# Another order of all engines for one attention kernel on one core

## The chip, the cores and the metric

The kernel runs on one core of a Trainium2 chip. A time is the device time of one execution in microseconds (us); of several, the median is given. The core has five engines that run their own instruction streams and wait for each other by semaphores: TensorE (PE in the profile, its weight loads apart as PEld), VectorE (DVE), ScalarE (ACT), GpSimd (POOL) and SyncE (SP). Transfers are issued by the last two, and a few by ScalarE.

## The reference

Four batches of eight heads, 1024 positions, 64 values per head; float32 in and out.

```python
scale = 1.0 / np.sqrt(head_dim)
scores = scale * np.matmul(q, k.transpose(0, 1, 3, 2))
scores = scores + bias
scores_max = np.max(scores, axis=-1, keepdims=True)
attn = np.exp(scores - scores_max) / (np.sum(np.exp(scores - scores_max), axis=-1, keepdims=True) + 1e-8)
return np.matmul(attn, v).astype(np.float32)
```

## The kernel before

The 32 heads are taken in 16 pairs, in two groups of nine and seven pairs. The work is cut into 256 slots: one head, one block of 128 queries, all 1024 keys. A slot's scores fill two PSUM banks, and three slots (a round) fill the six banks of the tile `pl` (position 0, 1 or 2 in the round says which banks). So a slot can be filled only when the slot three before it in the same position has been read.

No maximum is subtracted. ScalarE takes exp of 227 slots from PSUM to bf16 (line 398), as a rule one slot of 1024 columns per instruction; in a few rounds three slots go in two instructions of 1536 columns. VectorE does the other 29 in six steps (fixed, frac, square, shift, cube, last) that build the bits of a bf16; the first reads the two PSUM banks. TensorE then multiplies the exponentials with v, eight matmuls per slot (line 461), v having a column of ones so that the sum comes along. Up to seven slots share one PSUM bank `po`; VectorE takes its reciprocal (`rs`), scales it (`ob`), and the result is stored from the SP queue. Two such banks, tags xa and xb, alternate, and the transposes of q and k use the same two.

The bias is added once per chunk of queries, when a chain of heads starts: for later heads TensorE adds the difference to the scores that are still in PSUM. For that each pair needs q and k transposed, and once more with the other head's negated: `ko`, `qo` (copied out of PSUM), `ke`, `qe` (half of a pair and half of the next, copied by VectorE for the early pairs, by a transfer for later ones). Early pairs' k and q are first set beside each other in the tile `side`, of which there is one buffer. Loads are issued by GpSimd and convert to bf16; the tiles of pair p are used again by pair p + 4.

What sets the order is a table, `ORDER`, of some 1430 words, one instruction or group each, read in a row; each engine executes its part of that row in that order. The words that the text uses, with a slot's number, or a pair's behind k, q or r:

- F, G: the first and second half of a slot's scores (four matmuls of 128 columns, or two of 256); X: a slot's exp on ScalarE; P, Q: the two wide ones of a round
- f r s h c l: the six steps of a slot on VectorE
- A: a slot's eight output matmuls; a letter a or b behind it opens a new bank with that tag; R, M: reciprocal and evacuation of a bank. `SIZES` says how many slots each bank holds
- S, T, C, D, N: set beside, transpose (with tag a or b), copy out, double on VectorE, negate; V: v's copy
- U, L: ask for the next load. For L it also waits for the VectorE instruction that stands last in the row:

```python
if kind in "LU":
    asked.append(vec.last if kind == "L" else None)
...
gate = asked.pop(0)
if gate is not None:
    tc.add_manual_dep(flight[i], gate.name, DATA, reason="issued beside VectorE's long steps")
```

Of the kernel before, what the change touches and what calls it, by code (L numbers as in the profile page):

```python
# [8 lines left out]
F32 = mybir.dt.float32  # L9
# [13 lines left out]
Dq4p1 F24 X23 G24 Cq5 F25 A13 A16 X24 Dq5p1 G25 Dq5p0 F26 G26 Sk6 A19 X25 f26 F27 G27 Tk6a X27 F28 Ck6 G28 A18 F29
X28 Sq6 G29 F30 R2 G30 M2 Tq6a X29 r26 F31 A21b G31 X30 Cq6 F32 G32 A20 V4 X31 A22 f32 F33 G33 Tk7a X33 F34 Dk6p0 G34
F35 Dq6p0 X34 A28 Ck7 G35 F36 G36 s26 X35 Tq7a F37 Cq7 A27 X36 A29 G37 h26 A23 F38 c26 X37 A24a G38 Dq6p1 F39 A25 X38
R3 V5 F40 G39 Dq7p0 G40 Dq7p1 A30 X39 A35 Dk7p0 F41 M3 A34 X40 G41 l26 A33 Tk8b X41 F42 G42 Ck8 F43 G43 X42 F44 f43
G44 Tq8b X44 F45 G45 Cq8 A31 F46 X45 F47 Dk8p0 G46 Dq8p0 A26b G47 X46 V6 F48 R4 G48 f47 A36 X48 A41 F49 G49 A40 M4
X49 F50 G50 Sr0 F51 r43 G51 X50 A39 Tr0a F52 Cr0 A38 X51 F53 G53 Dr0p3 G52 r47 A37 X53 F54 Dq6p2 G54 R5 X52 F56 Sr1
s43 G56 X54 Tr1a r32 F55 Cr1 X56 G55 Dr0p1 F57 M5 G57 X55 F59 s47 A56a G59 A42 X57 Dr1p1 F58 Dr1p0 G58 f59 A44 X58
A46 F60 G60 A45 s32 X60 F61 G61 h43 A49b R6 F62 h32 X61 G62 c43 F63 G63 A48 X62 r59 L U F64 G64 M6 L A52 A50 X64 c32  # L30
A51 F65 s59 A53 X63 A54a G65 R7 L U U U h47 A55 F67 l32 X65 G67 F66 A60 G66 X67 A62 M7 F68 G68 A61 X66 f68 F70 G70
A63 A58b X70 F69 R8 G69 l43 F71 X69 G71 F73 G73 A67 c47 X71 A57 F72 M8 G72 A66 l47 X72 F74 G74 X73 h59 F75 G75 f74
A47 A65 X75 F76 G76 A64 r74 L U U X76 F77 G77 F78 c59 G78 X77 A73a F79 l59 G79 A72 X79 A70 F80 G80 A69 X78 f80 F82
G82 A43 A75 X82 F81 R9 G81 M9 L F83 G83 X81 F85 f83 G85 A76 A71b X85 F84 G84 r80 L U A81 X84 F86 G86 r68 A78 F88 X86
s74 G88 F87 G87 s68 A59 X87 A82 F89 h68 A77 R10 G89 s80 L U X88 A79 F90 c68 G90 X89 R11 M10 F91 G91 X90 l68 F92 X91
G92 M11 L F93 A89a h80 X92 G93 h74 A68 A84 c74 A85 X93 F94 G94 r83 A86 A90 X94 c80 F95 G95 F96 A32 X95 G96 R12 F97
s83 A93b A87 P96 M12 G97 F98 G98 l74 A88 Tq9a Q96 F99 G99 h83 A92 A91 c83 F100 X99 A74 Cq9 G100 A94 F101 X100 Dq8p1
G101 R13 F102 M13 L Tk9a X101 F103 l80 G102 G103 A96b X102 A101 F104 Ck9 L G104 A97 X103 f104 F105 G105 Tk10a X105
F106 Ck10 G106 F107 G107 X106 Nq9 F108 G108 f107 A80 X108 A100 F109 G109 l83 A95 X109 F110 G110 A99 F111 X110 R14
G111 M14 F112 Tq10a r104 P111 G112 A103b Cq10 L F113 G113 A108 r107 A98 Q111 Tq11a Nq10 F114 Cq11 G114 F115 A106 X114  # L40
s107 L G115 F116 G116 Nq11 A109 X115 s104 F117 G117 Tk12a h104 X117 F118 Ck12 G118 A105 A102 X118 f116 F120 G120
Tk11a X120 F121 Ck11 L G121 F119 G119 X121 F123 f119 G123 A110a A114 X123 F124 G124 R15 F122 M15 X124 G122 F126 c104
L G126 A113 X122 Tq12b r116 F127 G127 X126 s116 L A111 A83 A112 h107 L F125 X127 Cq12 A115 G125 F129 R16 G129 X125
M16 L U F130 G130 c107 Tk13b X129 F128 l104 G128 A121a A126 X130 A123 l107 F132 A127 X128 A117 G132 A120 h116 A118
X132 Ck13 F131 G131 F133 R17 G133 X131 M17 L F135 G135 A124b f135 L X133 F134 G134 A122 A130 X134 r119 F138 G138 F136
X138 G136 F137 f136 L U U U G137 Tk14a X137 F141 G141 A129 Ck14 X141 F139 F140 c116 G139 A137 X139 Tq14a G140 Cq14
F144 X140 F142 G142 l116 L G144 A131 X142 A125 F143 R18 G143 M18 A104a X144 F145 G145 r135 A107 X145 A133 s119 F147
A128 A116 r136 X143 G147 A134 s135 F148 A132 X147 G148 h119 F146 R19 L G146 Nq12 A139b X148 M19 F150 G150 c119 Tq13a
X146 F151 Cq13 L A138 A143 X150 G151 l119 F149 A140 A141 X151 F153 G149 h135 Tq15a s136 L X149 F154 G154 Nq13 G153
A142 Nq14 L X154 F152 Cq15 G152 A119 X153 f152 F157 G157 A148a A145 X157 F156 r152 L G156 F155 G155 X156 R20 F160  # L50
f155 G160 A144 A149 X160 F159 G159 s152 L A147 X159 F158 G158 M20 F163 A146 c135 X158 G163 F162 G162 r155 A156 X163
# [12 lines left out]
G216 A207b F218 X216 A208 l199 G218 A206 F217 X218 F219 G217 c203 G219 A210 X217 R29 F221 f219 G221 A211 X221 F220
G220 M29 F222 G222 X220 F224 f222 G224 A212 A213 X224 F223 G223 r219 F225 X223 G225 F227 r222 A220a A216 X225 s222
F226 G226 A215 h222 G227 P226 F228 R30 s219 A214 G228 A221 M30 A209 Q226 A217 A224b R31 F229 l203 G229 F230 A198 X229
G230 A218 M31 F231 G231 X230 c222 F232 G232 A223 f231 A199 X232 F233 G233 A228 l222 X233 F234 G234 F235 G235 X234
F236 f235 G236 A225 A233a X236 F237 G237 R32 h219 F238 X237 r235 F239 G238 A203 r231 A234 P238 G239 M32 F240 G240
A226 s235 A227 Q238 F241 c219 F242 G241 s231 A232 A222 P241 h235 F243 G243 R33 c235 G242 A239b A238 l219 Q241 A229
A230 F244 G244 l235 F245 A240 X244 G245 F246 G246 M33 A237 X245 F247 f246 G247 A243 A235a X247 F248 G248 h231 A219  # L70
X248 R34 F249 r246 G249 F250 G250 s246 X249 A236 F251 A242 h246 A245 P250 M34 G251 F252 G252 c231 A244 A241 A247b
Q250 l231 F253 F254 A248 G253 A249 R35 c246 X253 F255 G254 M35 A251 G255 X254 l246 A252 A231 A250 X255 A253a R36 A246
M36 A254 A255 R37 M37
"""
SIZES = (6, 7, 7, 7, 7, 7, 5, 6, 6, 7, 7, 7, 7, 7, 7, 7, 7, 7, 7, 7, 7, 7, 7, 7, 7, 7, 7, 7, 7, 5, 7, 7, 7, 7, 7, 7,
         7, 4)


class Recorder:

    def __init__(self, engine):
        self.engine, self.last = engine, None

    def __getattr__(self, name):
        def call(*args, **kwargs):
            i = getattr(self.engine, name)(*args, **kwargs)  # L86
            self.last = i.ins
            return i
        return call
# [3 lines left out]
def kernel(  # L93
# [610 lines left out]
```

## Time and profile before

| what | us |
|---|---|
| median of 3 runs (lowest, highest) | 225.54 (225.21, 225.86) |
| the profiled execution | 225.5 |
| its span, first to last instruction | 223.7 |
| TensorE busy | 214.4 |
| ScalarE busy | 211.9 |
| VectorE busy | 204.9 |
| GpSimd busy | 70.8 |

Busy time of TensorE is modelled, since its matmuls are pipelined; ScalarE's instructions overlap their neighbours by some tenths of a microsecond, so a mean duration is longer than the distance from start to start. A row of a group ends with the idle time of the engine just before the group's instructions and what ended it. The helper that records VectorE's instructions gives all of them line 86, so they are told apart by their tiles.

### The profile page before, as it was taken

To read this page: it belongs to the slowest core of one execution; us is meant where nothing else is said; L and a number is where in the kernel's file an instruction comes from. 1 tells how busy PE (TensorE), PEld (TensorE's weight loads), DVE (VectorE), ACT (ScalarE), POOL (GpSimd) and SP (SyncE) were. 2 spreads that over 40 slices of the span, in tenths; PEclk is the share of its full clock that TensorE was granted. 3 is DMA by queue.
4 is the path that set the end of the run, shared out by engine and by line. 5 is a ranking of instruction groups with operands and counts; after the bars stand their busy time and mean duration, and the time that the engine had idled before them with its cause. 6 is when DMAs were issued, how large, how long until landed. Compare 5 with 4: busy or idle time off the path is not lost.

```text
span 223.7 us, 9044 instructions
## 1 busy us (share of the span) xinstructions
PE 214.4 (96%) x3965; PEld 197.2 (88%) x3965; DVE 204.9 (92%) x354; ACT 211.9 (95%) x227; POOL 70.8 (32%) x90
## 2 busy tenths in 40 slices
PE   7799999999999999999999999999999999999992
PEld 2689989999999999999999889888898999898992
DVE  2679999999999999999998899999999999999992
ACT  2799998999999999999999999999999999999991
POOL 8825347446254555030436542343000000000000
PEclk9999999999999999999999999999999999999999
DMA  6999999999979999788999999999311021130123
GB/s 177 225 205 216 228 234 177 167 149 180 155 109 153 107 118 144 96 121 179 145 192 143 168 115 201 172 145 95 71 45 44 23 65 41 32 85 25 39 71 103
DMA packets 86087, 28.87 MB, mean 129 GB/s; under 512 B 65888, under 2 KB 82784, under 8 KB 86048
## 3 DMA queue, kind: packets, MB, share of 16 engines
q0 software_dynamic: 62880, 14.06, 70.2%
q1 hardware_dynamic: 22464, 13.38, 23.5%
q10 hardware_dynamic: 704, 0.85, 1.3%
q8 instruction: 31, 0.51, 1.0%
q14 instruction: 8, 0.07, 0.1%
HBM read 29.36 MB, written 8.39 MB: 169 GB/s over the span
## 4 chain that ended last, share of the span: by engine, by line
ACT 54%; PE 22%; DVE 11%; DMA 7%; issue 2%; SPq 1%; DVEq 0%
ACT E L398 54%; PE pl L375 12%; PE po L461 6%; DMA out_dram<-ob 3%; DMA dy<-in_k_dram 2%; PE px L276 2%; DMA ke<-ko 2%; DVE ds L86 1%; DVE qe L86 1%; PE pl L372 1%; DVE ko L86 1%; DVE ob L86 1%; DVE side L86 1%; DVE de L86 1%; DVE qo L86 1%
## 5 line engine op out<-in xcount | busy, mean ns | idle before, releaser
L398 ACT ACTIVATE E<-pl 128x1024 bf16<-128x1024 f32 (+2 forms) x223 | 209.0, 1102 | 2.7 <-PE pl L375 2.5
L461 PE MATMUL po<-vall,E 128*128 128x65 bf16 x1816 | 87.5, 194 | 0.7 <-DVE ob L86 0.3
L461 PEld LDWEIGHTS <-E 128*128 128x128 bf16 x1816 | 77.4, 98 | 3.5 <-DVE ob L86 0.9
L375 PE MATMUL pl<-qo,ko 128*128 128x128 bf16 (+1 forms) x752 | 78.1, 239 | 0.6 <-ACT E L398 0.5
L375 PE MATMUL pl<-qe,ke 128*128 128x128 bf16 (+1 forms) x648 | 67.3, 239 | 0.7 <-ACT E L398 0.3
L375 PEld LDWEIGHTS <-ko 128*128 128x128 bf16 x856 | 57.3, 98 | 6.2 <-ACT E L398 2.1
L375 PEld LDWEIGHTS <-ke 128*128 128x128 bf16 x648 | 43.3, 98 | 4.3 <-ACT E L398 1.6
L86 DVE TENSOR_SCALAR dy<-pl 128x1024 int32<-128x1024 f32 x29 | 35.3, 1218 | 3.1 <-PE pl L375 2.9
L86 DVE SCALAR_TENSOR_TENSOR de<-dy,ds 128x1024 uint16<-128x1024 int32 x29 | 34.9, 1214 | 0.1
L213 POOL DMA_DIRECT2D k<-in_k_dram x18 | 16.3, 909 | 28.8 <-PE pl L375 8.2
L86 DVE TENSOR_TENSOR ob<-po,rs 128x448 f32<-128x448 f32 (+3 forms) x38 | 22.8, 599 | 0.4
L213 POOL DMA_DIRECT2D q<-in_q_dram x18 | 16.6, 921 | 20.4 <-DVE ds L86 10.1
L250 POOL DMA_DIRECT2D vall<-in_v_dram x18 | 16.2, 903 | 18.4 <-DMA vall<-in_v_dram 8.0
L86 DVE TENSOR_TENSOR ds<-ds,de 128x1024 f16<-128x1024 f16 x29 | 19.6, 680 | 0.1
L86 DVE TENSOR_TENSOR ds<-de 128x1024 f16<-128x1024 f16 x29 | 19.5, 676 | 0.1
L86 DVE TENSOR_SCALAR de<-dy 128x1024 f16<-128x1024 uint16 x29 | 19.5, 682 | 0.1
L372 PE MATMUL pl<-ident,braw 128*128 128x128 bf16 x136 | 14.1, 228 | 0.0
L86 DVE TENSOR_SCALAR qo<-px,sgn 128x1024 bf16<-128x1024 bf16 (+2 forms) x18 | 12.4, 688 | 1.6 <-PE px L276 1.4
L461 PE MATMUL po<-vall,de 128*128 128x65 bf16 x232 | 12.5, 194 | 0.0
L86 DVE TENSOR_SCALAR de<-de 128x1024 f16<-128x1024 f16 x29 | 12.3, 432 | 0.2
L372 PEld LDWEIGHTS <-braw 128*128 128x128 bf16 x136 | 11.7, 149 | 0.5
L86 DVE COPY ko<-px 128x1024 bf16<-128x1024 bf16 (+1 forms) x16 | 10.6, 666 | 1.2 <-PE px L282 1.1
(54 smaller groups left out, 127.2 us busy)
## 6 DMA issues: line engine op xcount, KB each, us to landing
ke<-ko SPq DMA_DIRECT2D x20, 128.0 KB, 5.5
k<-in_k_dram POOLq DMA_DIRECT2D x18, 128.0 KB, 5.2
q<-in_q_dram POOLq DMA_DIRECT2D x18, 128.0 KB, 4.5
vall<-in_v_dram POOLq DMA_DIRECT2D x18, 128.0 KB, 5.6
out_dram<-ob SPq DMA_DIRECT2D x33, 64.0 KB, 2.9
braw<-in_bias_dram POOLq DMA_DIRECT2D x7, 256.0 KB, 6.0
de<-in_v_dram POOLq DMA_DIRECT2D x7, 256.0 KB, 7.4
out_dram<-ob SPq DMA_DIRECT2D x9, 192.0 KB, 4.1
```

The source lines that it names most:

```text
L86: i = getattr(self.engine, name)(*args, **kwargs)
L213: return nc.gpsimd.dma_start(out=t[:, :, y, :], in_=(qf, kf)[x][pr][:, y].rearrange("p (c d) -> p c d", d=D))
L250: return nc.gpsimd.dma_start(out=vall[:, (2 * pr + t) % VR, :, :D], in_=vf[pr][:, t])
L276: m = nc.tensor.transpose(px[:, c, :], raws[pr, which, c0][:, c].rearrange("p t d -> p (t d)"), ident[:])
L372: m = nc.tensor.matmul(to, braw[:, c1, :].rearrange("p (kp kc) -> p kc kp", kc=NCH)[:, kc, :], ident8[:], start=i == 0 and order[0] == "b" ...
L375: m = nc.tensor.matmul(pl[:, 2 * x + b, i * P:(i + n) * P], kk[:, kc, :], qq[:, c:c + n, :].rearrange("p c q -> p (c q)"), start=i == 0 an ...
L398: read(nc.scalar.activation(E[:, e0:e0 + n].rearrange("p b x -> p (b x)"), pl[:, b0:b0 + n].rearrange("p b x -> p (b x)"), ACTF.Exp, scale ...
L461: nc.tensor.matmul(bank[b][:, banks[b].index(s), :], weights(s, kc), vall[:, slots[s][2] % VR, kc, :], start=first and kc == 0, stop=kc == ...
```

## The change

`ORDER` is another row of nearly the same words, and three banks hold other numbers of slots; the rest of the program is the same, word for word. The slots on VectorE are the same but two: 48 in place of 47 and 224 in place of 222. Rounds 96 and 111 take three exponentials in place of two wide ones. The words that ask for loads are 27 L and 48 U in place of 29 L and 46 U. The description of the change speaks of a search for the mean end over nine courses with drawn disturbances, and of 24 of 42 loads that wait for VectorE; in the built program 27 of these 42 have a wait for VectorE, and before it was 29. Of the table's lines these hold places that the prediction speaks of:

```diff
-Dq1p0 X2 F6 Sk2 G6 Tk2a X6 F5 G5 Sq2 F7 X5 G7 Dk1p1 Tq2b X7 Cq2 F8 G8 F9 G9 V0 X8 F10 Ck2 A0b A2 X9 Dq1p1 A3 Sk3 G10
+Dq1p0 X2 F6 Sk2 G6 Dk1p1 Tk2a X6 F5 Ck2 G5 F7 X5 Sq2 F9 G7 Dq1p1 G9 Dk2p0 X7 F8 G8 Tq2b V0 X8 F10 Cq2 G10 A5a A2 X9
...
-A128 A116 r136 X143 G147 A134 s135 F148 A132 X147 G148 h119 F146 R19 L G146 Nq12 A139b X148 M19 F150 G150 c119 Tq13a
+G145 A107 X145 A133 s135 F147 A132 M18 G147 X143 A131 F148 l116 A138 G148 X147 F146 A134 G146 R19 Tq13a X148 M19 F150
...
-SIZES = (6, 7, 7, 7, 7, 7, 5, 6, 6, 7, 7, 7, 7, 7, 7, 7, 7, 7, 7, 7, 7, 7, 7, 7, 7, 7, 7, 7, 7, 5, 7, 7, 7, 7, 7, 7,
+SIZES = (6, 7, 7, 7, 7, 7, 6, 4, 7, 7, 7, 7, 7, 7, 7, 7, 7, 7, 7, 7, 7, 7, 7, 7, 7, 7, 7, 7, 7, 5, 7, 7, 7, 7, 7, 7,
```

The first place is VectorE's preparation of pairs 1 and 2. `k16_127` and `q16_129` are the loads of k2 and q2, `ko_294` is k1, `qo_325` is q1. Before:

```order
L86 COPY side_333<-k16_127 128x2x8x64
L86 COPY side_357<-q16_129 128x2x8x64
L86 COPY ke_368<-ko_294 64x1024
L86 TENSOR_SCALAR qo_380<-px_370,sgn_91 128x1024
L86 COPY vall_98<-de_131 128x16x64
L86 COPY ko_404<-px_339 128x1024
```

And now:

```order
L86 COPY side_333<-k16_127 128x2x8x64
L86 COPY ke_339<-ko_294 64x1024
L86 COPY ko_355<-px_341 128x1024
L86 COPY side_368<-q16_129 128x2x8x64
L86 TENSOR_SCALAR qe_378<-qo_325 64x384
L86 COPY ke_339<-ko_355 64x1024
L86 COPY vall_98<-de_131 128x16x64
L86 TENSOR_SCALAR qo_409<-px_394,sgn_91 128x1024
```

k1's doubled copy and k2's copy out of PSUM now stand between the two copies that set k2 and q2 beside.

The second place is the same for pair 4: `k16_217` and `q16_219` are its loads, `ko_481` or `ko_475` is k3. Before:

```order
L86 COPY ke_406<-ko_481 64x1024
L86 TENSOR_TENSOR ob_534<-po_408,rs_517 128x384
L86 TENSOR_SCALAR qo_545<-px_524,sgn_91 128x1024
L86 COPY side_561<-k16_217 128x2x8x64
L86 TENSOR_SCALAR qe_442<-qo_545 64x1024
L86 COPY side_594<-q16_219 128x2x8x64
L86 COPY ko_609<-px_576 128x1024
```

And now:

```order
L86 TENSOR_TENSOR ob_524<-po_415,rs_508 128x384
L86 TENSOR_SCALAR qo_536<-px_515,sgn_91 128x1024
L86 COPY side_555<-k16_217 128x2x8x64
L86 COPY ke_357<-ko_475 64x1024
L86 TENSOR_SCALAR qe_453<-qo_536 64x1024
L86 TENSOR_SCALAR qe_586<-qo_536 64x1024
L86 COPY ko_596<-px_576 128x1024
L86 COPY side_617<-q16_219 128x2x8x64
```

k3's doubled copy, which stood ahead of the evacuation, a second copy of q3 and k4's copy out now stand between the two.

The third place is VectorE at slots 80 and 83: their first steps write `dy_1901` and `dy_1949` before, `dy_1908` and `dy_1956` now, and `dy_1796` (now) is slot 74. Before:

```order
L86 TENSOR_SCALAR dy_1901<-pl_102 128x1024
L86 RECIPROCAL rs_1926<-po_1711 128x7
L86 TENSOR_TENSOR ob_1930<-po_1711,rs_1926 128x448
L86 TENSOR_SCALAR dy_1949<-pl_102 128x1024
L86 TENSOR_SCALAR de_1975<-dy_1901 128x1024
```

And now:

```order
L86 TENSOR_SCALAR dy_1908<-pl_102 128x1024
L86 TENSOR_TENSOR ob_1933<-po_1713,rs_1841 128x448
L86 TENSOR_SCALAR de_1945<-dy_1796 128x1024
L86 TENSOR_SCALAR dy_1956<-pl_102 128x1024
L86 TENSOR_SCALAR de_1988<-dy_1956 128x1024
```

The reciprocal has gone ahead of slot 80's first step, and slot 74's second step stands ahead of slot 83's first one.

More of the change, by code (lines that the diff above doesn't have):

```diff
@@ L23 @@
[L23 to L27, printed above, removed]
@@ new lines @@
+X28 Ck6 F29 G29 F30 R2 Dk6p0 G30 X29 F31 M2 Tq6b V4 G31 X30 F32 Cq6 G32 A20a f32 X31 A21 F33 G33 Tk7b X33 Dq6p1 F34
+G34 Dq6p0 A23 Ck7 X34 F35 G35 A28 r26 F36 X35 G36 Dk7p0 F37 G37 s26 Tq7b X36 A27 Cq7 A22 A29 X37 F38 V5 G38 F39 R3
+Dq7p0 G39 X38 A25b h26 F40 M3 G40 A34 X39 c26 A24 F41 A30 Dq7p1 X40 A31 l26 G41 Tk8a X41 F42 F43 Ck8 G42 G43 X42 A26
+f43 F44 G44 Tq8a X44 F45 Cq8 G45 F46 X45 G46 Dk8p0 F47 A35 Dq8p0 A33a V6 X46 G47 F48 R4 G48 M4 A41 X47 F49 Sr0 G49
+f48 A40 A36 X49 F50 G50 Tr0b r43 X50 A38 F51 Cr0 G51 F52 X51 A39 Dr0p3 Dq6p2 F53 G53 r48 A37 X53 G52 F54 R5 r32 G54
@@ new lines @@
+X52 Sr1 F56 s43 G56 X54 Dr0p1 F55 s32 Tr1b X56 M5 G55 F57 h43 G57 X55 Cr1 F59 G59 A42a Dr1p0 A56 X57 Dr1p1 F58 h32
+G58 f59 A46 X58 A44 F60 G60 A45 c32 X60 F61 G61 s48 A47 F62 X61 A54b R6 L U r59 G62 A49 F63 M6 L X62 F64 G64 l32 A50
+X64 A55 G63 A53a h48 A62 X63 F65 R7 c43 G65 F67 G67 M7 X65 A61 c48 L U U A51 A52 F66 s59 X67 G66 F68 G68 A60 X66 f68
+L F70 G70 A58 A63b X70 F69 l43 G69 F71 A57 X69 G71 F73 l48 A67 X71 F72 G72 A66 r68 G73 X72 F74 R8 h59 G74 X73 F75 f74
+L G75 A65 X75 A48 F76 G76 M8 A64 X76 F77 R9 G77 s68 A73a F78 X77 G78 c59 L F79 G79 A69 l59 L U X79 A70 F80 G80 A76
@@ new lines @@
+X78 f80 F82 G82 A72 A75 X82 F81 M9 G81 F83 r74 G83 X81 F85 G85 f83 A43 A71b X85 F84 G84 A81 r83 X84 F86 G86 A78 Dq8p1
+L U F88 X86 s74 G88 F87 G87 s83 A82 X87 A79 h74 L F89 G89 h68 L U A77 X88 A59 F90 R11 R10 c74 G90 X89 F91 M10 G91 X90
+l74 F92 X91 G92 M11 A32a F93 r80 X92 G93 A87 A91 s80 F94 X93 G94 A85 h83 F95 c68 G95 X94 A92 A74 c83 A84 F96 X95 h80
+G96 A89b R12 F97 M12 G97 X96 F98 c80 A90 G98 X97 A86 l68 A88 F99 G99 X98 Tq9a A94 Cq9 F100 X99 G100 A93 l80 A68 F101
+X100 G101 F102 Tk9a R13 X101 M13 G102 F103 Nq9 L G103 A96b X102 Ck9 L F104 G104 A101 f104 A97 X103 F105 G105 Tk10a
@@ new lines @@
+X105 l83 F106 G106 F107 G107 X106 F108 f107 G108 A80 A100 X108 F109 G109 Ck10 A99 X109 F110 G110 r107 A95 F111 X110
+R14 G111 M14 A98a F112 A106 r104 X111 G112 Tq10b A103 X112 Cq10 F113 G113 A109 F114 Nq10 X113 G114 s107 Tq11b F115
+X114 Cq11 G115 F116 G116 h107 L A108 X115 F117 f116 L U G117 Tk12b X117 F118 G118 Ck12 A105 A102 X118 F120 R15 G120
+s104 Tk11b X120 F121 M15 G121 F119 Ck11 L G119 X121 F123 G123 f119 A83a A112 X123 F124 G124 Tq12b c107 X124 F122 Cq12
+G122 F126 A110 X122 l107 L U G126 A114 F127 X126 G127 A113 r119 F125 A111 X127 G125 s119 Tk13b F129 h104 X125 G129
@@ new lines @@
+G150 h135 A141b X146 h136 F151 G151 Cq13 L U U A139 A116 X150 c136 F149 G149 A140 l119 X151 F153 Tq15a X149 F154 Cq15
+G154 G153 A142 Nq13 X154 F152 Nq15 G152 A143 f152 A119 X153 F157 G157 A147a X157 c135 F156 G156 F155 G155 X156 F160
+f155 G160 A145 A144 X160 F159 G159 R20 A146 Nq14 X159 F158 r155 G158 A149 F163 r152 L U U X158 F162 G163 M20 A151
+G162 X163 s155 A148 F161 R21 A153b M21 X162 F166 G166 l135 A156 A150 X166 G161 Tk15a h155 L F165 X161 Ck15 G165 F169
+G169 c155 A159 X165 A161 F164 G164 X169 F168 f164 G168 A154 A160 X168 F172 G172 s152 A162a X172 F167 G167 h152 F171
@@ new lines @@
+l136 A157 X167 G171 A165 F175 G175 c152 X171 A158 F170 R22 A163 M22 G170 X175 A166 A167 l155 F174 A169b X170 G174
+F178 l152 A171 X174 F173 G178 G173 R23 A168 X178 f173 F177 G177 A172 X177 F181 M23 G181 F176 G176 X181 F180 f176 G180
+A152 A175 X180 F184 G184 r173 A174 X184 F179 G179 r176 F183 A181a r164 X179 A178 G183 F187 s173 X183 G187 R24 s176
+F182 G182 X187 h173 A170 F186 s164 G186 X182 c173 F190 A179 M24 X186 F185 l173 G185 A180 A155 X185 G190 F189 h164
+G189 A177 X190 h176 F188 c176 G188 X189 c164 A136b A135 R25 F193 l164 X188 G193 F192 A184 G192 X193 F191 l176 G191
@@ new lines @@
+A187 A185 X191 F196 G196 A183 f196 X192 F194 G194 A186 X194 F195 M25 G195 F199 R26 G199 X195 F197 f199 G197 A182a
+A193 X197 F198 G198 F202 f198 G202 F200 X202 G200 r196 A173 X200 F201 G201 r199 F205 G205 X201 M26 A164 F203 A190
+s199 A189 X205 F204 r198 G204 A192 s196 G203 X204 F208 G208 f203 A194b A188 X208 F207 G207 A197 R27 h196 X207 F206
+G206 M27 F211 A201 h199 X206 A191 s198 G211 A202 F210 r203 X211 A200 G210 A205a c196 A204 X210 F213 l196 G213 F209
+A176 X213 F212 G212 c199 A196 X212 A195 G209 l199 F215 X209 G215 F214 R28 R29 s203 X215 G214 h198 F216 X214 M28 G216
@@ new lines @@
+M29 F218 X216 A211b h203 F217 c198 G218 A210 X218 G217 l198 A207 F219 G219 X217 F221 G221 f219 A212 A208 X221 F220
+G220 c203 F222 X220 G222 F224 r219 G224 A206 X222 f224 F223 G223 A213 A220a X223 F225 R30 r224 G225 A215 X225 F227
+l203 F226 G226 A214 P226 F228 s224 A222 G228 G227 h224 A216 Q226 A221 M30 A209 F229 c224 G229 A218b R31 F230 X229
+l224 G230 F231 G231 A228 X230 F232 f231 G232 A199 A217 X232 F233 G233 s219 F234 A223 X233 M31 G234 F235 r231 G235
+X234 F236 G236 f235 A198 A203 X236 F237 G237 A225a r235 X237 F238 F239 h219 G238 A224 R32 s235 P238 G239 A227 F240
```

61 lines of the change are left out of this document (13 added, 48 removed).

## The prediction

> **What bounds the kernel now.** I read the page's busy shares first, then ScalarE's timeline over the whole span, and then two stretches of that timeline in which nothing is late.
>
> ```profile
> PE 214.4 (96%) x3965; PEld 197.2 (88%) x3965; DVE 204.9 (92%) x354; ACT 211.9 (95%) x227; POOL 70.8 (32%) x90
> PEclk9999999999999999999999999999999999999999
> ```
>
> ```profile
> 8.40 4.10 ACT L398 ACTIVATE E<-pl 128x512 bf16<-128x512 f32 x6 [0.77 <-PE pl L375]
> 12.78 21.29 ACT L398 ACTIVATE E<-pl 128x1024 bf16<-128x1024 f32 x23 [0.28 <-PE pl L375]
> 34.50 3.77 ACT L398 ACTIVATE E<-pl 128x1024 bf16<-128x1024 f32 x4 [0.43 <-PE pl L375]
> 38.54 8.36 ACT L398 ACTIVATE E<-pl 128x1024 bf16<-128x1024 f32 x9 [0.27 <-PE pl L375]
> 47.33 125.89 ACT L398 ACTIVATE E<-pl 128x1024 bf16<-128x1024 f32 x135 [0.43 <-PE pl L375]
> 173.54 45.72 ACT L398 ACTIVATE E<-pl 128x1024 bf16<-128x1024 f32 x46 [0.32 <-PE pl L375]
> ```
>
> ```profile
> 51.98 7.44 ACT L398 ACTIVATE E<-pl 128x1024 bf16<-128x1024 f32 x8
> 81.27 9.33 ACT L398 ACTIVATE E<-pl 128x1024 bf16<-128x1024 f32 x10
> 90.33 2.95 ACT L398 ACTIVATE E<-pl 128x1536 bf16<-128x1536 f32 x2
> ```
>
> ```profile
> L398 ACT ACTIVATE E<-pl 128x1024 bf16<-128x1024 f32 x207 | 191.9, 1087 | 1.8 <-PE pl L375 1.7
> L398 ACT ACTIVATE E<-pl 128x1536 bf16<-128x1536 f32 x12 | 17.1, 1543 | 0.0
> ```
>
> Three engines are nearly full, at full clock, and ScalarE is the one that ends the program. Its exponentials overlap: eight in a row take 7.44 us, so with 1.09 for the last one they start (7.44 - 1.09) / 7 = 0.91 us apart; ten take 9.33, 0.92 apart. The wide one starts about 2.95 - 1.54 = 1.4 before the next. I take 0.91 and 1.4. Against that pace ScalarE loses more than its idle time shows:
>
> - 12.78 to 47.33: 34.55 us for 36 starts, 36 x 0.91 = 32.8, so 1.8 lost
> - 47.33 to 173.54: 126.2 us for 135 starts, four of them wide, 131 x 0.91 + 4 x 1.4 = 124.8, so 1.4 lost
> - 173.54 to the last start, 45.72 - 1.09 = 44.6 us for 45 starts, eight of them wide, 37 x 0.91 + 8 x 1.4 = 44.9, so nothing
>
> Some 3.2 us in all, 1.4% of the profiled execution's 225.5 (its span is 223.7, and it is one of those near the median of 225.54). All that an order can win lies there, unless it also shortens the first 12.8 us, which it leaves alone. Each gap's releaser is a score matmul; what made that late is in the chain of waits, in VectorE's busy time by stretch (columns: stretch, its length, busy time) and in VectorE's timeline.
>
> ```profile
> 23.04 0.46 PE px L276 x8
> 23.53 0.53 DVE side L86
> 24.06 0.60 DVE ko L86
> 24.69 0.64 DVE ke L86
> ...
> 35.06 0.57 DVE side L86
> 35.67 0.62 PE px L276 x8
> ```
>
> ```profile
> 15.60:23.60 8.00, 7.29 (x18) 1.00 1.24 214
> 23.60:35.60 12.00, 11.74 (x23) 1.00 1.45 216
> 35.60:47.30 11.70, 11.43 (x23) 1.00 1.54 167
> ```
>
> ```profile
> 14.16 0.43 DVE L86 COPY side<-q 128x1024 bf16<-128x1024 bf16 x1 [0.96 <-DMA q<-in_q_dram]
> 22.34 0.42 DVE L86 COPY side<-k 128x1024 bf16<-128x1024 bf16 x1
> 22.67 0.41 DVE L86 TENSOR_SCALAR qe<-qo 64x1024 bf16<-64x1024 bf16 x1
> 23.53 0.53 DVE L86 COPY side<-q 128x1024 bf16<-128x1024 bf16 x1 [0.44 <-PE px L276]
> ```
>
> From 23.5 to 35.6 us the chain is VectorE alone, 11.74 of 12.00 us busy: it prepares pairs 3 to 6, and then TensorE's transposes wait for its side copies. Just ahead of that it sat idle for 0.44 us, because there is one side buffer: q4's copy waits until k4's transposes have read it.
>
> **The change, part by part.** TensorE's 3965 and VectorE's 354 instructions stay the same in kind and number, and no byte is moved more or less. So the sum starts at zero and holds only waits, and two exponentials more.
>
> *Two exponentials more: +0.1.* Rounds 96 and 111 take three of 1024 columns in place of two of 1536. By starts 6 x 0.91 - 4 x 1.4 = -0.1; by durations 6 x 1.087 - 4 x 1.543 = +0.35. I take +0.1, between them.
>
> *VectorE's preparation, 12 to 47 us: -0.7.* The wait of 0.96 us at 14.2 for q2's load now has k1's copy and k2's copy out ahead of it, 0.64 + 0.60 us by the chain's rows at 24.69 and 24.06. But the chain from 15.7 to 23.5 is TensorE's, so this alone buys nothing. The wait of 0.44 us at 23.53 gets k3's doubled copy and a second of q3 into it, 0.64 and 0.41 us by the rows at 24.69 and 22.67; it stands at the head of VectorE's stretch, so 0.4 of it should come out at 34.5 us. In the next 24 us VectorE idles 0.26 + 0.27 us more, of which the new order may win half. The bound on the good side is all that idle time, 0.71 + 0.26 + 0.27 = 1.2 us, since as much VectorE work stands ahead of the first queries of pair 8 as before (all preparations up to there are the same). On the other side stands q2: its copy and transposes come one exponential later, and if that is late it costs one part of a fill, 0.4. Ends -1.2 and +0.4.
>
> *VectorE's own slots at 62 to 83 us: +0.3.* A slot done on VectorE holds its two PSUM banks until its first step has read them, and TensorE can refill them only then.
>
> ```profile
> 76.79 1.23 DVE L86 TENSOR_SCALAR dy<-pl 128x1024 int32<-128x1024 f32 x1 [0.36 <-PE pl L375]
> 77.93 0.20 DVE L86 RECIPROCAL rs<-po 128x7 f32<-128x7 f32 x1
> 78.16 0.62 DVE L86 TENSOR_TENSOR ob<-po,rs 128x448 f32<-128x448 f32 x1
> 78.95 1.22 DVE L86 TENSOR_SCALAR dy<-pl 128x1024 int32<-128x1024 f32 x1 [0.17 <-PE pl L375]
> ```
>
> ```profile
> 17.00 0.77 PE po L461 x24
> 129.28 0.22 PE pl L375 x2
> L86 DVE TENSOR_SCALAR de<-dy 128x1024 f16<-128x1024 uint16 x29 | 19.5, 682 | 0.1
> L86 DVE TENSOR_TENSOR ob<-po,rs 128x448 f32<-128x448 f32 x32 | 19.7, 617 | 0.4
> ```
>
> These are slots 80 and 83. Now slot 74's second step (0.68) stands ahead of slot 83's first one, and the reciprocal (0.20) no longer does: 0.48 later, less the 0.17 it waited, makes 0.31. TensorE has three outputs (0.77 / 3 = 0.26 each) and four half fills (0.22 each) between that slot and the refill, 1.66 us against the step's 1.22: room for 0.44. It just fits, with 0.1 left. VectorE is as tight at slots 68, 74 and 80, and by the same count of instructions has up to 0.7 us more work ahead of them than before; one overhang of 0.3 is what I charge. Ends 0, and four overhangs, +1.2.
>
> *Between 83 and 174 us: -0.4.* One swap can be priced. Ahead of q13's transposes VectorE's evacuation of bank 19 stood, and TensorE waits there; the group's row has it:
>
> ```profile
> L276 PE MATMUL px<-ident,q 128*128 128x128 bf16 x72 | 5.5, 219 | 0.3 <-DVE ob L86 0.3
> ```
>
> In the new order the transposes come first and take bank 18's place, which a long step and a reciprocal separate from its evacuation: 0.3 won. Bank 19 is then wanted three half fills and eight transposes later, 3 x 0.22 + 0.46 = 1.1 us, for 0.20 + 0.62 of VectorE: covered. The wait of 0.32 us at 173.54 has slots 196, 199 and 198 in one row before and after; only the work between their first steps is exchanged (0.68 for 0.62), so I count 0.1. Of the 1.4 us lost on the whole stretch, 0.4 is what I can point at. Ends: -1.2, nearly all of it, and +0.5, as much again as the two places that I trust.
>
> *Loads: -0.1.* 27 of the 42 wait for VectorE, before it was 29 (the words of the change say 24). What differs is what they run beside. A load's issue holds GpSimd for 0.91 us, and short copies then take longer (columns: least, median and most ns):
>
> ```profile
> L213 POOL DMA_DIRECT2D k<-in_k_dram x18 | 16.3, 909 | 28.8 <-PE pl L375 8.2
> L86 DVE TENSOR_SCALAR de<-de x29: 372/420/784, 41.8 to 213.2; 128x1024 f16<-128x1024 f16 x29
> L86 DVE TENSOR_SCALAR q<-qo x7: 408/419/699, 98.8 to 147.6; 128x1024 bf16<-128x1024 bf16 x7
> L86 DVE TENSOR_SCALAR de<-de 128x1024 f16<-128x1024 f16 x29 | 12.3, 432 | 0.2
> ```
>
> Counting the VectorE instructions that follow each gate within 1.1 us, ten of these short ones stood beside a gated load and now two do. The mean is 0.012 us over the median for the 29 of the second row, 0.35 us in the run; so eight fewer are worth 0.1 to 0.4 of VectorE's time, of which some reaches the end. Ends -0.4 and 0. [...] A load that comes too late is the other side: q15's second half waits for q14's copy out, some eight exponentials ahead of its transposes, 8 x 0.91 = 7.3 us against 0.9 to issue and this to land:
>
> ```profile
> q<-in_q_dram POOLq DMA_DIRECT2D x18, 128.0 KB, 4.5
> ```
>
> *The end: 0.* The last bank holds the same four slots, and the same output and evacuation follow the last exponential.
>
> Sum: +0.1 - 0.7 + 0.3 - 0.4 - 0.1 = -0.8, and 225.5 - 0.8 = 224.7 us.
>
> **The rivals.**
>
> *The idle time only moves: 225.6.* VectorE's preparation is a chain through one side buffer and two PSUM tiles, so what is filled at 23.5 us may be waited for at the next transposes; then the preparation and the middle give 0, and +0.1 stays. For it: as much VectorE work as before stands ahead of pair 8's first scores. Against it: that work had 1.2 us of idle time in it.
>
> *The slots on VectorE hold their banks too long: 226.8.* The four first steps at 62 to 83 us overrun their room of 0.44 us; each holds up a fill and ScalarE behind it, 4 x 0.31 = 1.2 us, and nothing is won before, since the stretch until 47 us is VectorE's in both. It decides as soon as slot 83's first step comes more than 0.44 us later against its fill than now. For it: 0.31 of that is already spent. Against it: the waits of 0.36 and 0.17 at these steps show that VectorE is the early one there.
>
> *Nearly all is won: 223.2.* Preparation -1.2, middle -1.2, +0.1. For it: every gap in ScalarE has a late VectorE instruction behind it. Against it: 92% busy, VectorE has no room to be early everywhere.
>
> **How the numbers follow.** Forecast 0.45, with a range of its own from 224.1 to 225.3; only moved 0.22; slower 0.23; nearly all 0.10. The measurement tells 0.3%, 0.68 us, from no change, so faster means under 224.86. Two thirds of the forecast's chance lies there, with all of the last rival and a little of the first: 0.30 + 0.10 + 0.02 = 0.42. Slower, over 226.2: most of the second rival and a little of the first, 0.19 + 0.02 = 0.21. Within: 0.37. From 223.4 to 226.7 the range leaves out half of the last rival and half of the slower one, with what I have not thought of.
>
> **What would show it.** Right: ScalarE's gaps at 34.5 and 38.5 gone and the exponential that started at 47.33 starting 0.4 or more earlier; VectorE's waits for q's load and for transposes before 24 us under 0.5 us together; no idle time of q's transposes for VectorE's evacuation; a maximum of VectorE's short steps under 0.6 us after 75 us. Wrong: a new gap of ScalarE between 62 and 83 us; a wait of TensorE for a first step there; a gap at an exponential where there was none before. The forecast falls if the start of the exponential at 47.33 doesn't move, since it carries most of the sum.

## The result and the profile after

| kernel | median us (lowest, highest; executions) | ratio to the kernel before [95% interval] |
|---|---|---|
| new order, first timing | 224.51 (224.12, 225.36; 6) | 0.9939 [0.9913, 0.9964] |
| the kernel before beside it | 225.88 (225.21, 226.6; 7) | |
| new order, repeated | 224.83 (224.31, 226.3; 12) | 0.9974 [0.9952, 0.9996] |
| the kernel before beside it | 225.70 (224.45, 227.44; 35) | |

By the ratios the new order is faster by 0.6% (1.4 us) in the first timing and by 0.3% (0.6 us) in the repeat, against 0.8 us predicted. The medians differ by 1.4 and 0.9 us. A seventh execution of the first timing, in which TensorE was slow throughout (287 ns for a matmul with v, against 194 in the other profiles, and busy for 526.3 us), took 533 us and is left out, so the profile after is that of the repeat: 225.07 us, span 223.3. Its busy shares and ScalarE's timeline, in the columns of the same views of before:

```profile
PE 215.5 (97%) x3965; PEld 198.7 (89%) x3965; DVE 203.6 (91%) x354; ACT 211.5 (95%) x229; POOL 71.0 (32%) x90
```

```profile
9.42 0.60 ACT L398 ACTIVATE E<-pl 128x512 bf16<-128x512 f32 x1 [1.74 <-PE pl L375]
10.19 3.41 ACT L398 ACTIVATE E<-pl 128x512 bf16<-128x512 f32 x5 [0.17 <-PE pl L375]
13.87 158.91 ACT L398 ACTIVATE E<-pl 128x1024 bf16<-128x1024 f32 x173 [0.27 <-PE pl L375]
173.10 45.71 ACT L398 ACTIVATE E<-pl 128x1024 bf16<-128x1024 f32 x46 [0.32 <-PE pl L375]
```

```profile
L398 ACT ACTIVATE E<-pl 128x1024 bf16<-128x1024 f32 x213 | 196.3, 1104 | 0.7 <-PE pl L375 0.6
L398 ACT ACTIVATE E<-pl 128x1536 bf16<-128x1536 f32 x8 | 11.3, 1518 | 0.0
```

The gaps at 34.5, 38.5 and 47.3 us are gone; between 13.87 and 173.10 no idle time is long enough to start a new row. But this execution also began late: its first exponential of 1024 columns starts at 13.87, that of before at 12.78. From that exponential to the last gap it is 173.10 - 13.87 = 159.23 us, before 173.54 - 12.78 = 160.76: 1.53 less, of which 1.09 was spent ahead of it. What follows the last gap takes 45.71 us, before 45.72. Of the two other traces with these words (below), the one with the longer warm-up has no gap between either; the one without gates has 0.43 us at 47.0, one exponential later than the gap before. The late start comes back below, under the warm-up.

VectorE, where most of the gain was expected, at pair 4 and in its waits between 13 and 24 us (line waited for, on what, total, times, longest), first now and then before:

```profile
22.81 0.42 DVE L86 COPY side<-k 128x1024 bf16<-128x1024 bf16 x1
23.14 0.62 DVE L86 COPY ke<-ko 64x1024 bf16<-64x1024 bf16 x1
23.68 0.86 DVE L86 TENSOR_SCALAR qe<-qo 64x1024 bf16<-64x1024 bf16 x2
24.57 0.69 DVE L86 COPY ko<-px 128x1024 bf16<-128x1024 bf16 x1
25.30 0.43 DVE L86 COPY side<-q 128x1024 bf16<-128x1024 bf16 x1
...
DVE qo L86 <- PE px L276: 0.6, 1, 0.6
DVE rs L86 <- PE po L461: 0.4, 1, 0.4
DVE ko L86 <- PE px L276: 0.4, 1, 0.4
```

```profile
DVE side L86 <- DMA q<-in_q_dram: 1.0, 1, 1.0
DVE qo L86 <- PE px L276: 0.5, 2, 0.4
DVE side L86 <- PE px L276: 0.4, 1, 0.4
```

Between the two side copies of pair 4 VectorE now works without a pause, where it waited 0.44 us. The wait of 1.0 us for q2's load is gone too; two waits for transposes stay.

### The profile page after: what moved, and what is told of

The parts are those of the page before. It is cut to its first block, busy times and chain, and to the rows that moved or that the text cites. A ratio compares the mean times of both kernels' runs of the same rounds, so it can differ in the third digit from the quotient of the medians.

```text
span 531.5 us, 9048 instructions
## 1 busy us (share of the span) xinstructions
PE 526.3 (99%) x3965; PEld 441.0 (83%) x3965; DVE 206.5 (39%) x354; ACT 234.1 (44%) x229; POOL 68.7 (13%) x90
## 4 chain that ended last, share of the span: by engine, by line
PE 99%; DVE 0%; issue 0%
PE pl L375 57%; PE po L461 30%; PE px L276 7%; PE pl L372 4%; PE pl L518 1%; PE px L282 0%; PE pl L276 0%; DVE ob L86 0%; DVE E L86 0%; DVE rs L86 0%; DVE warm L86 0%
## 5 line engine op out<-in xcount | busy, mean ns | idle before, releaser
L398 ACT ACTIVATE E<-pl 128x1024 bf16<-128x1024 f32 (+2 forms) x225 | 231.2, 1031 | 285.5 <-PE pl L375 280.7
L461 PEld LDWEIGHTS <-E 128*128 128x128 bf16 x1816 | 170.2, 150 | 22.0
L461 PE MATMUL po<-vall,E 128*128 128x65 bf16 x1816 | 180.2, 287 | 0.0
L375 PE MATMUL pl<-qo,ko 128*128 128x128 bf16 (+1 forms) x752 | 178.8, 438 | 0.0
L375 PE MATMUL pl<-qe,ke 128*128 128x128 bf16 (+1 forms) x648 | 154.9, 436 | 0.0
L375 PEld LDWEIGHTS <-ko 128*128 128x128 bf16 x856 | 119.4, 166 | 26.0 <-ACT E L398 0.2
L375 PEld LDWEIGHTS <-ke 128*128 128x128 bf16 x648 | 90.6, 166 | 21.4
L372 PE MATMUL pl<-ident,braw 128*128 128x128 bf16 x136 | 28.1, 383 | 0.0
L461 PEld LDWEIGHTS <-de 128*128 128x128 bf16 x232 | 22.1, 150 | 2.3
L375 PE MATMUL pl<-qz,ko 128*128 128x128 bf16 (+1 forms) x72 | 21.0, 454 | 0.0
```

Source lines behind the costliest of these rows:

```text
L372: m = nc.tensor.matmul(to, braw[:, c1, :].rearrange("p (kp kc) -> p kc kp", kc=NCH)[:, kc, :], ident8[:], start=i == 0 and order[0] == "b" ...
L375: m = nc.tensor.matmul(pl[:, 2 * x + b, i * P:(i + n) * P], kk[:, kc, :], qq[:, c:c + n, :].rearrange("p c q -> p (c q)"), start=i == 0 an ...
L398: read(nc.scalar.activation(E[:, e0:e0 + n].rearrange("p b x -> p (b x)"), pl[:, b0:b0 + n].rearrange("p b x -> p (b x)"), ACTF.Exp, scale ...
L461: nc.tensor.matmul(bank[b][:, banks[b].index(s), :], weights(s, kc), vall[:, slots[s][2] % VR, kc, :], start=first and kc == 0, stop=kc == ...
```

## The experiments

All kernels below compute the whole result. The starts of the exponentials in each trace give the distances used here: from slot 5 to slot 50 (preparation and its end), 50 to 85 (VectorE's slots at 62 to 83 us), 85 to 139, 139 to 153 (around q13's transposes), 153 to 200. One execution each, in us:

| trace | slot 5 starts | 5 to 50 | 50 to 85 | 85 to 139 | 139 to 153 | 153 to 200 |
|---|---|---|---|---|---|---|
| before | 14.60 | 38.30 | 26.56 | 45.70 | 12.11 | 37.21 |
| new order | 15.70 | 36.82 | 26.63 | 45.83 | 11.84 | 37.22 |
| new order, longer warm-up | 14.67 | 36.62 | 26.64 | 45.83 | 11.85 | 37.22 |
| new order, no gates | 14.41 | 37.18 | 26.70 | 45.83 | 11.85 | 37.22 |
| first part only | 14.61 | 37.78 | 26.56 | 45.71 | 11.95 | 37.39 |
| third part only | 14.46 | 38.14 | 26.54 | 45.90 | 11.84 | 37.33 |
| before, longer warm-up | 14.42 | 38.83 | 26.59 | 45.71 | 12.11 | 37.12 |

Up to slot 50 the first three kernels of the new order have the same words, so their rows show how far single executions differ: 36.62 to 37.18 us. Four traces have the order before up to slot 48 (the second and third parts are two of them): 38.14 to 38.83.

**The new order as it is.** Its edit is the whole change.

> The changed kernel itself, for a trace to read. By the prediction: ScalarE's gaps at 34.5 and 38.5 us of the order before are gone, and the exponential that started at 47.33 us (slot 42) starts 0.4 us or more earlier; VectorE waits under 0.5 us for q2's load and for transposes before 24 us; between 62 and 83 us one late fill of about 0.3 us. Time 224.7 us, 0.8 below the kernel before. By the rival that idle time only moves: slot 42 starts within 0.2 us of 47.33, and the time lost on the way to 47 us comes out as a wait at a later transpose.

Measured: the second half of the first table, and the second row here. 5 to 50 is 1.5 us shorter, 139 to 153 0.27 shorter, 85 to 139 0.13 longer (the two exponentials more), the rest the same.

**One part of the new order at a time.** The row of words was cut at slots 48, 110 and 199, where both orders have nearly the same work behind them, and one part was taken from the new order, the rest from before. Where a bank's tag had to fit, a and b were exchanged in the rest of the row; the second part takes the three bank sizes along. The first differing words of each:

```diff
 first part, to the scores of slot 48
-Sk2 G6 Tk2a X6 F5 G5 Sq2
+Sk2 G6 Dk1p1 Tk2a X6 F5 Ck2 G5
 second part, to the scores of slot 110
-R4 G48 f47 A36 X48 A41
+R4 G48 M4 A41 X47 F49 Sr0 G49 f48 A40 A36 X49
 third part, to slot 199
-G109 l83 A95 X109 F110 G110 A99 F111
+G109 l83 A99 X109 F110 G110 r107 A95 F111
```

> The new order up to the first scores of slot 48 (about 51 us), the order before behind it; all of the loads' gates and both rounds of wide exponentials as before. By the prediction this part holds most of the gain: -0.7 us against the kernel before, visible in the trace as an earlier start of the exponential of slot 42 and of all that follow it. By the rival that idle time only moves: 0 within 0.3 us, slot 42 at the same time. A third reading: the start of slot 42 comes earlier, but the later order, planned for the later start, gives it back by waiting: then the end is within 0.3 us although slot 42 is 0.4 us or more early.

> The order before up to slot 48, the new order from there to the scores of slot 110 (about 51 to 102 us), and the order before again. It holds slots 68, 74, 80 and 83 on VectorE, seven of the gates that no longer stand beside short copies, and round 96 with three exponentials. By the prediction: +0.3 for a first step that holds its banks too long, +0.05 for the exponential, up to -0.1 for the gates: +0.2 us. By the rival that these slots hold up ScalarE four times: +1.2 us. If the gates carry the gain: -0.4 us.

> The order before up to the scores of slot 110, the new order from there to slot 199 (about 102 to 173 us), and the order before again; q13's transposes ahead of bank 19's evacuation is in it. By the prediction: -0.4 us, and TensorE no longer waits at q13's transposes. If the gain is all in the preparation before 47 us: 0. If ScalarE's small losses on this stretch (1.4 us from 47 to 173) are won: -1.0 us.

Measured: first part 224.98 us, ratio 0.9972 [0.9949, 0.9995]; second 225.90, 0.9993 [0.9968, 1.0019]; third 225.84, 1.0020 [1.0000, 1.0041]. Only the first has an interval that lies below 1: it gains 0.6 us by its ratio. ScalarE's timeline with the first part, and with the third:

```profile
12.78 34.29 ACT L398 ACTIVATE E<-pl 128x1024 bf16<-128x1024 f32 x37 [0.27 <-PE pl L375]
47.46 125.27 ACT L398 ACTIVATE E<-pl 128x1024 bf16<-128x1024 f32 x134 [0.39 <-PE pl L375]
173.05 45.71 ACT L398 ACTIVATE E<-pl 128x1024 bf16<-128x1024 f32 x46 [0.32 <-PE pl L375]
```

```profile
38.20 8.37 ACT L398 ACTIVATE E<-pl 128x1024 bf16<-128x1024 f32 x9 [0.39 <-PE pl L375]
46.78 4.71 ACT L398 ACTIVATE E<-pl 128x1024 bf16<-128x1024 f32 x5 [0.21 <-PE pl L375]
51.69 121.17 ACT L398 ACTIVATE E<-pl 128x1024 bf16<-128x1024 f32 x131 [0.20 <-PE pl L375]
173.28 45.71 ACT L398 ACTIVATE E<-pl 128x1024 bf16<-128x1024 f32 x46 [0.43 <-PE pl L375]
```

With the first part the gaps before 47 us are gone, and a gap of 0.39 remains at 47.46, with one exponential more ahead of it than before. By the starts it is 1.06 us ahead of before at slot 36, 0.92 at slot 41, and 0.52 at slot 50: half of what the preparation won is given back by then. That is one trace: slots 41 to 50 take 7.45 us in it and 7.05 to 7.64 in the four traces of the order before. The third part, which changes nothing before 102 us, has gaps at 38.2 and 46.8 as the order before has them, has the q13 stretch at 11.84 as the new order has, and is no faster: its median is 0.1 us above that of the kernel before, and its interval begins at 1.0000, so the 0.4 us that the prediction gave it is not there. In its trace 85 to 139 is 0.20 us longer, 139 to 153 0.27 shorter and 153 to 200 0.12 longer. The profiled execution of the second part (227.08 us) was its slowest, with a wait of VectorE for a late load, and is not read for stages:

```profile
57.58 0.51 DVE L86 COPY side<-qrest 128x640 bf16<-128x640 bf16 x1 [0.97 <-DMA qrest<-in_q_dram]
```

**The first part cut again.** Up to slot 12, slots 12 to 29, slots 29 to 47; and pair 4's place alone in the order before:

```diff
-V1 F14 R0 G14 Dk3p0 Tq3a
+V1 F14 R0 G14 Tq3a
...
-Sk4 G16 A8 Dq3p0 Tk4a X15 A7 Sq4 F17 X16 A11 Ck4 G17
+Sk4 Dk3p0 G16 A8 Dq3p0 Tk4a Dq3p1 X15 A7 F17 X16 A11 Ck4 Sq4 G17
...
-Tq4a Dq3p1 V2
+Tq4a V2
```

> The new order up to the exponential of slot 12 (about 20 us), the order before behind it: the wait for q2's load is filled with k1's and k2's copies. By the prediction this alone buys nothing, since TensorE carries the chain there: from slot 5's exponential to slot 41's 31.1 to 31.3 us as in the order before (three traces: 31.25, 31.13, 31.08), and the time within 0.2 us of it. If filling VectorE's early idle time is what matters: 0.5 us less by slot 41.

> The new order from slot 12 to slot 28 (about 20 to 36 us) alone: the wait of 0.44 us between the side copies of k4 and q4 is filled here. By the prediction the head of VectorE's stretch: from slot 5 to slot 41 0.4 us less, 30.7. If the part carries all that the first 51 us showed: 30.3. If every part only works with the others: 31.1 to 31.3.

> The new order from slot 29 to slot 46 (about 36 to 51 us) alone: slot 26's steps on VectorE stand later behind pair 7's preparation. The prediction gave this stretch half of VectorE's idle time there, 0.3 us: 30.9 from slot 5 to slot 41. If the gain is the order in which VectorE serves slot 26 and the preparation, and not the waits ahead of 24 us: 30.5 or less.

> The order before with one edit: k3's doubled copy, q3's second one and k4's copy out stand between the side copies of k4 and q4, as in the new order. By the prediction VectorE's wait of 0.44 us at 23.5 us is gone and ScalarE wins 0.4 us by slot 41 (30.7 from slot 5). By the rival that idle time only moves: the wait at 23.5 is gone, another of about that length stands before 36 us, and slot 41 stays at 31.1 to 31.3.

Measured, beside a median of 225.87 us of the kernel before (the last three columns are from the profiled execution):

| new words | median us | ratio [95% interval] | its time | slots 5 to 41 | 5 to 50 |
|---|---|---|---|---|---|
| up to slot 12 | 225.71 | 1.0015 [0.9982, 1.0047] | 227.52 | 31.25 | 38.43 |
| slots 12 to 29 | 225.72 | 1.0009 [0.9984, 1.0035] | 224.46 | 30.38 | 37.42 |
| slots 29 to 47 | 225.41 | 0.9992 [0.9961, 1.0023] | 227.51 | 31.10 | 38.20 |
| pair 4's place alone | 225.88 | 0.9998 [0.9971, 1.0024] | 226.18 | 30.55 | 37.36 |

No interval lies below 1. The stretch from slot 5 to slot 41, which the expectations name, says more. In the six traces that have pair 4's copies where they were before, it takes 31.07 to 31.44 us; in the seven that have them in the new place (the two in this table, the first part, and all others with that part in them), 30.12 to 30.55. The two groups do not overlap, and one edit, pair 4's place, is enough to change from one to the other. A late start does not do it: of the pieces that began late (1.2 to 1.8 us after the order before), pair 4's place alone is in the short group, and the pieces up to slot 12 and at slots 29 to 47 are in the long one. VectorE and ScalarE with pair 4's place alone:

```profile
23.39 0.42 DVE L86 COPY side<-k 128x1024 bf16<-128x1024 bf16 x1
...
24.96 0.69 DVE L86 COPY ko<-px 128x1024 bf16<-128x1024 bf16 x1
25.68 0.43 DVE L86 COPY side<-q 128x1024 bf16<-128x1024 bf16 x1
```

```profile
14.00 33.41 ACT L398 ACTIVATE E<-pl 128x1024 bf16<-128x1024 f32 x36 [0.30 <-PE pl L375]
47.62 88.23 ACT L398 ACTIVATE E<-pl 128x1024 bf16<-128x1024 f32 x94 [0.21 <-PE pl L375]
```

The wait ahead of q4's copy is gone, and so are the gaps at 34.5 and 38.5: up to slot 41 the mechanism works as the prediction had it. The times do not show it. Each ratio is known to about 0.3%, 0.6 us, so a gain of that size can hide in the interval of pair 4 alone; the interval of slots 12 to 29 ends at a gain of 0.4. One profiled execution is not a typical one either: that of slots 12 to 29 is the fastest of its ten, and those up to slot 12 and of slots 29 to 47 are the slowest of theirs. Which piece of the first part carries its gain in time stays open.

**No gates.** All 27 words L of the new order become U, so that no load has a gate.

```diff
-X65 A61 c48 L U U A51 A52
+X65 A61 c48 U U U A51 A52
```

> The new order with no load waiting for VectorE: all 42 loads of pairs 9 to 15 issue as soon as their tile and the loads ahead allow. By the prediction the gates keep GpSimd's issues away from VectorE's short copies: without them some ten short steps after 52 us take up to 0.8 us, VectorE loses 0.3 to 1 us and the end comes 0.1 to 0.5 us later. If the gates don't decide that (the new order's own trace has seven slow steps after 52 us with gates): within 0.2 us of the new order, and as many slow steps.

Measured: 224.53 us, 0.9949 [0.9926, 0.9972], not told apart from the time with gates. The short steps in both (columns: least, median and most ns), with gates and then without:

```profile
L86 DVE TENSOR_SCALAR de<-de x29: 369/419/789, 43.7 to 213.3; 128x1024 f16<-128x1024 f16 x29
L86 DVE TENSOR_SCALAR q<-qo x7: 374/415/786, 95.2 to 140.4; 128x1024 bf16<-128x1024 bf16 x7
```

```profile
L86 DVE TENSOR_SCALAR de<-de x29: 374/420/793, 42.8 to 212.4; 128x1024 f16<-128x1024 f16 x29
L86 DVE TENSOR_SCALAR q<-qo x7: 376/427/789, 94.4 to 139.5; 128x1024 bf16<-128x1024 bf16 x7
```

The slowed steps are there either way. Of all VectorE instructions after 52 us, four took over 0.1 us more than the median of their like in the profile of before; in the new order's it was six, and nine without gates. There are more of them, not fewer, and the time does not follow.

**A longer warm-up.** The matmuls on zeros that run ahead of the data become 13 in place of 10, in the new order and in the one before; and in a third kernel together with the first part of the new order and q13's transposes moved ahead of bank 19's evacuation.

```diff
-        for i in range(10):
+        for i in range(13):
             wrote(nc.tensor.matmul(pl[:, 4, :], zeros[:, :P], zeros, start=True, stop=True), 4)
```

> The new order with 13 warm-up matmuls in place of 10, so that TensorE is busy until about 6.7 us, when its first operands come. In four of nine traces its first matmuls run at half speed for 1.1 to 1.8 us longer (314 ns against 223 for one with the bias). If that late start is what spreads the times, and if the new order takes up most of it (its own trace started 1.1 us late and was level by slot 41): the late start is gone from the trace and the median falls by 0.2 us or less against the new order's 224.8. If the new order passes the late start on: 224.3 or less.

> The order before with 13 warm-up matmuls in place of 10. If the order before passes a late start on to its end: 0.5 to 0.8 us less than the kernel before (half the executions win 1.1 to 1.8). If it takes it up as well, by loads that are there earlier relative to its work: 0.2 us less or nothing. Then the two orders still differ by what the first part of the new one wins, 0.5 us or more.

> What the traces point to as the best: the new order up to slot 48, the order before behind it with one edit, q13's transposes ahead of the negation of q12 and the evacuation of bank 19, both rounds of wide exponentials, and 13 warm-up matmuls. If the gain is the first part's and that of the slots around 149 (0.2 to 0.3 us at slot 153 in the traces of the new order): equal to the new order with the longer warm-up, or 0.2 us under it. If the rest of the new order carries something that the first part needs: 0.5 us above it.

Measured: new order 224.46 us (223.94 to 225.28), 0.9939 [0.9916, 0.9962], the lowest median of all; order before 225.66, 0.9989 [0.9964, 1.0014]; the third 225.59, 0.9992 [0.9969, 1.0015]. The new order's gain is not told apart from its gain without the longer warm-up. The third was not the test that it was meant to be. In the order before, q13's transposes use the tag of bank 19 itself, so moving them ahead of that bank's evacuation in the row makes them wait for all of it. TensorE's timeline in that kernel, and ScalarE behind it:

```profile
132.23 0.61 PE L276 MATMUL px<-ident,q 128*128 128x128 bf16 x8 [0.94 <-DVE ob L86]
...
133.10 40.52 ACT L398 ACTIVATE E<-pl 128x1024 bf16<-128x1024 f32 x44 [0.58 <-PE pl L375]
```

In the new order bank 19 has the other tag, and q13 takes bank 18's place. TensorE there, and below it in the order before:

```profile
131.39 0.61 PE L276 MATMUL px<-ident,q 128*128 128x128 bf16 x8
```

```profile
132.68 0.61 PE L276 MATMUL px<-ident,q 128*128 128x128 bf16 x8 [0.29 <-DVE ob L86]
```

So the swap needs the exchange of tags with it: the stretch 139 to 153 took 11.84 us with it, and 12.70 without, 0.6 more than before. Nor is the wait there in every execution of the order before: in two of eight traces with its words in this stretch, those of the second part and of slots 12 to 29, the transposes do not wait, and the stretch takes 11.85 us as in the new order. The other six take 11.95 to 12.40.

## Why the prediction was right, step by step

- *Two exponentials more, +0.1*: right. Slots 85 to 139, which hold rounds 96 and 111, took 0.13 us longer in all three traces of the whole new order. Other words differ in this stretch too, so it is not the exponentials alone.
- *VectorE's preparation, -0.7*: the right place and cause, and too small for the whole order. Slot 42's start was to move by 0.4 or more; it moved from 47.33 to 46.77 in an execution that began 1.1 us late. From slot 5 to slot 50 the three traces of the new order gain 1.1 to 1.7 us over the 38.30 of before. The first part alone gains 0.6 us by its ratio. The cause is shown up to slot 41 by pair 4's place alone, 0.7 us shorter there than before, where 0.4 was forecast for it. The rival that *the idle time only moves* could hold for half of the first part's gain, 0.92 us ahead at slot 41 and 0.52 at slot 50, but slots 41 to 50 scatter by as much.
- The sign *VectorE's waits for q's load and transposes before 24 us under 0.5 us* failed, though the load's wait went: 0.6 and 0.4 us remain at the transposes. The gaps closed in spite of them, so it was not a condition.
- *VectorE's slots at 62 to 83 us, +0.3*: the term was mis-sized. Slots 50 to 85 took 0.07 to 0.14 us longer, ScalarE has no gap there, and no matmul waited for a first step (one weight load did, for 0.2 us, in two of the three traces). The overhang that I charged stayed within the 0.44 us of room; the rival of late banks is wrong with it.
- *83 to 174 us, -0.4*: too large, and the third part alone does not show it. The q13 swap was priced right against the execution that the prediction read. The idle time of q's transposes for VectorE's evacuation went from 0.3 us to none:

```profile
L276 PE MATMUL px<-ident,q 128*128 128x128 bf16 x72 | 5.5, 219 | 0.0
```

  and the stretch 139 to 153 is 0.26 to 0.27 us shorter in three traces. But where the order before has no such wait, in two of eight traces, there is nothing to win. The 0.1 at 173 us failed: the gap of 0.32 stands as before.
- *Loads, -0.1*: wrong. The step that failed is the count of short instructions that follow a gate, ten before and two now. The maximum of short steps after 75 us was to fall under 0.6 us and is 0.79, and without any gate the time is no longer. All six slow instructions of the new order's trace (at 53.7, 80.0, 83.0, 116.1, 135.9 and 140.6 us) run beside a load's issue on GpSimd of 0.9 to 1.0 us. Which of these loads had a gate was not read; a count of gates does not see where the others fall.
- *The end, 0*: right, 45.71 us for 45.72.

The sum of -0.8 lies between the two measured gains, 0.6 us and 1.4 us by the ratios, and that is in part luck. Two large errors lie on one side, a preparation that won more and almost no cost at 62 to 83 us; two smaller ones (0.1 at 173 us and 0.1 for the loads, neither won) lie on the other. In the traces the gain is larger than forecast: from slot 5 to the start of the last exponential the three of the new order take 201.8 to 202.4 us, and before took 203.6. The parts measured alone add to 0.6 + 0.2 - 0.5 = 0.3 us by their ratios, with about 0.55 us of uncertainty each; that is compatible with the 0.6 us of the whole beside them, and does not show whether the parts help each other. In their traces, the whole new order has slots 5 to 50 in 36.6 to 37.2 us where the first part alone has 37.78, with the same words up to slot 48. There VectorE waited 1.2 us for v's loads (the seven copies of v; the idle time stands last):

```profile
L86 DVE COPY vall<-de 128x1024 bf16<-128x1024 bf16 x7 | 3.3, 469 | 1.2 <-DMA de<-in_v_dram 1.2
```

Why v's loads were later in that execution is open, and they are not the whole reason: the third kernel with the longer warm-up has the same words up to slot 48, no wait at these copies, and still takes 37.66 us.

## What to carry to other kernels

An order is worth reading at the engine behind the gaps: here VectorE's wait of 0.44 us at one side buffer, filled with copies that were due anyway, closed ScalarE's gaps at 34.5 and 38.5 us. A move gains only in a context that fits: q13's transposes moved ahead without their tag cost 0.6 us in its trace. An edit worth less than 0.3% can show in traces and not in a median, so its mechanism and its gain are two questions; and a wait that one trace shows may be missing in the next, so several traces of one order are worth more than one. A wait is not a term of the sum because a row names it; what counts is whether the exponential behind it starts earlier.

## What the runs showed of the hardware

*TensorE's first microseconds differ from execution to execution.* Ahead of the slots the program is the same in every order, and yet the same eight matmuls took 223 ns each before and 314 ns in the new order's profiled execution (columns: least, median and most ns, stretch), first before, then the new order, then the new order with 13 warm-up matmuls. By the starts the eight take up 0.50 us before and 0.86 in the new order, and the four transposes behind them 0.22 and 0.42: 0.58 and 0.52 of the speed, where an expectation above says half:

```profile
L372 PE MATMUL pl<-ident,braw x8: 223/225/228, 7.3 to 7.7; 128*128 128x128 bf16 x8
```

```profile
L372 PE MATMUL pl<-ident,braw x8: 314/314/314, 7.5 to 8.2; 128*128 128x128 bf16 x8
```

```profile
L372 PE MATMUL pl<-ident,braw x8: 223/224/228, 7.3 to 7.8; 128*128 128x128 bf16 x8
```

Four of ten traces with 10 warm-up matmuls had the slow ones and began 1.1 to 1.8 us late (first exponential at 9.4 to 9.9 us, the others at 8.2 to 8.4); none of three with 13 did. Not all of that is the slow matmuls: in two of the four, TensorE's first matmul on data also came late, at 6.8 us against 6.1 to 6.4 in the others, and so it did in one of the three with 13, whose first exponential came at 8.9. In the new order with 13 the whole run to the last gap then stands 1.2 us earlier:

```profile
12.85 158.72 ACT L398 ACTIVATE E<-pl 128x1024 bf16<-128x1024 f32 x173 [0.27 <-PE pl L375]
171.88 45.71 ACT L398 ACTIVATE E<-pl 128x1024 bf16<-128x1024 f32 x46 [0.32 <-PE pl L375]
```

Against 173.10 that is 1.22 us in one trace, the fastest of its twelve executions, and 0.37 us between the medians, which were not taken side by side; the order before got no faster by it. That the warm-up's length removes late starts is a pattern of 13 traces and not shown by the times. Nor was it shown what decides between the two speeds. In the stretches from 1.2 to 12.2 us the granted clock was 1.00 in the trace of before and in three of the four with slow matmuls, the new order's among them; in the fourth, of the piece at slots 29 to 47, it was 0.50 from 8.2 to 10.2 us.

*Short VectorE copies beside GpSimd's loads.* In the order before the seven copies of v went up to 853 ns, in the new order none above 416 (before, then new):

```profile
L86 DVE COPY vall<-de x7: 415/420/853, 16.1 to 50.2; 128x1024 bf16<-128x1024 bf16 x7
```

```profile
L86 DVE COPY vall<-de x7: 389/411/416, 16.9 to 50.0; 128x1024 bf16<-128x1024 bf16 x7
```

That is not the order alone: two more traces with these copies in the old order have at most 431 ns, and the new order without gates, which has the same words up to there, has 631. Added up over the copies and doublings of 1024 columns within SBUF before 52 us (`side`, `ke`, `qe`, `vall`), what they took over 0.42 us is 2.4 us before, 1.1 in the new order, 0.8 with the longer warm-up and 1.2 without gates. Within the four traces of the order before, though, it does not go with the time: the one with the least, 1.7 us, has the longest stretch from slot 5 to slot 50, 38.83. And the first part's trace has 1.9. So it is not shown that these delays carry any of the gain; they were not tried apart. The longest copy here, in the order before, ran from 29.63 us for 0.85 us, 0.43 over the median of its like, and beside it a load's issue held GpSimd from 29.37 us for 0.89.
